# A matrix product with a subtraction: rings of slots for loads and stores, listed transfers, and a second DMA queue

## The chip, the cores and the metric

The kernel runs on one core of one Trainium2 chip. The metric is the device time of one execution, in microseconds (us). Each core has five engines that run their own instruction streams in order: PE (TensorE, matrix products and transposes), DVE (VectorE), ACT (ScalarE), POOL (GpSimd) and SP (SyncE, which here only issues DMA transfers). The transfers themselves are carried out by the core's 16 DMA engines.

## The reference

```python
def setup_inputs():
    batch, m, k, n = 16, 512, 1024, 768
    return {
        "x": np.random.randn(batch, m, k).astype(np.float32),
        "weight": np.random.randn(k, n).astype(np.float32),
        "sub_value": np.random.randn(batch, m, n).astype(np.float32),
    }

def reference(x, weight, sub_value):
    return (np.matmul(x, weight) - sub_value).astype(np.float32)
```

Flattened, this is a product of 8192 x 1024 by 1024 x 768, less a matrix of 8192 x 768, all in float32. Through the DMA engines go x (33.6 MB), the weight (3.1 MB), sub (25.2 MB) and the output (25.2 MB), 87 MB in all.

## The kernel before

**Tiles.** The 8192 rows are cut into 64 m tiles of 128 rows. Eight m tiles make a block of 1024 rows: partition p of tile j of the block holds row 8p + j. So the rows of several neighbouring m tiles lie next to one another in memory, and one transfer of n tiles moves, for each partition, one contiguous row of n times 4 KB (x) or n times 3 KB (sub, out).

**One m tile's way.** The x tile arrives in float32. ACT casts it to float16 (`cast`, L99). Most tiles are then transposed by PE: four 128 x 128 transposes, in which a pair of float16 travels as one float32 (L116), and ACT copies the transposed tile from PSUM to SBUF (L123, called the xt copy below). The seven pairs of tiles whose first number is in `ON_DVE` (18, 24, 30, 36, 42, 48, 54) are transposed by DVE instead, 16 block transposes for a pair (L137). Then PE does 16 matmuls for a tile (L149), four for each of the four slices c of the inner dimension, into one of three PSUM buffers. DVE subtracts the sub tile from the PSUM buffer and writes the result over the sub tile in SBUF (`finish`, L160). The output is stored from there.

**Order of the work.** All instructions are kept in the order in which the program writes them, on each engine. The main loop (L218) runs over m tiles from 3 on. In the iteration of tile mi, PE does the matmuls of mi with the four transposes of tile mi + 2 between them, and ACT's copy of that tile follows. Then come the casts that are due: a tile of a DVE pair is cast seven tiles ahead, another four tiles ahead. Then `finish(mi)`, and, when a DVE pair comes up in six tiles, its 16 transposes are put on a list of which four are issued per iteration. So on ACT, the cast of a tile of a DVE pair stands before the xt copies of nearer tiles. The first three tiles are interleaved with the arrival of the four weight slices; idle matmuls (L177) fill the waits there.

**Transfers.** All transfers are issued on SP's queue. x lies in four buffers of four tiles each, sub and out in seven buffers of four tiles each (the weight's staging takes four of these first). The head is a written list: x tiles and weight slices, one by one, then x and sub by turns, one or two tiles each (L23). From then on the loop issues at each fourth tile an x load three groups ahead, a sub load two groups ahead and the store of the group two back, each of four tiles. A load waits on SP until the buffer that it fills is free, and every later transfer is behind it. The last group is stored in pieces of two, one and one tile (L244 to L246).

SP has eight completion semaphores for its transfers, which are used in rotation: each issue also waits until the transfer eight issues before it has landed.

## Time and profile before

| | |
|---|---|
| median of 8 runs | 213.15 us |
| lowest and highest | 212.65, 213.8 us |
| the profiled execution's own time | 212.65 us |
| its span, first to last instruction | 210.8 us |
| granted TensorE clock in it | 0.992 |
| moved by DMA | 87.23 MB, mean 414 GB/s |
| data and other packets | 9374, of them 1040 under 512 B |

The profile is of one execution. Its span is 1.85 us shorter than its time. Engine times in it are sums of busy time; waiting, branching and the issue of DMAs don't count as busy. A timeline line gives the start in us from the span's start, the duration, the engine (SPq is SP's queue), the line of the kernel, the operation, the tiles written and read, the shape, how many instructions were merged, and in brackets the idle time before with what ended it. A wait for several things is put down to the one that came last.

The transfers by kind, with the size of one and the median time from issue to landing:

```profile
x_tile<-in_x_dram SPq DMA_DIRECT2D x13, 2048.0 KB, 31.1
out_dram<-so_tile SPq DMA_DIRECT2D x15, 1536.0 KB, 31.9
so_tile<-in_sub_value_dram SPq DMA_DIRECT2D x14, 1536.0 KB, 33.0
```

A transfer issued in the middle of the kernel lands some 30 us later: it stands behind those issued before it.

### The profile page before, as it was taken

What the parts mean: (1) busy time and instruction counts of PE and PEld (TensorE: products, weight loads), DVE (VectorE), ACT (ScalarE), POOL (GpSimd) and SP (SyncE); (2) the same over time, 40 slices, a digit from 0 to 9 for tenths busy, and PEclk for the clock granted to TensorE, in tenths of its full rate; (3) what the DMA queues carried; (4) which work ended last, traced back from release to release, by engine and by line L of the source; (5) the groups of instructions that cost most, each with busy time, mean ns of one, the idle gap of its engine ahead of it and who ended that gap; (6) DMA issues with size and microseconds to landing.
All of it is one profiled execution on the core that took longest, in us unless ns stands there. A gap on an engine that the chain in (4) does not pass through costs nothing.

```text
span 210.8 us, 3028 instructions
## 1 busy us (share of the span) xinstructions
PE 198.5 (94%) x1249; PEld 129.9 (62%) x1249; DVE 114.0 (54%) x186; ACT 112.7 (53%) x115; POOL 0.7 (0%) x6
## 2 busy tenths in 40 slices
PE   7999799999999999999989999998999999999960
PEld 2455566776666775776656566664656666776630
DVE  0343313152598299389519939941993994133330
ACT  3646666757842847465086555509645553557300
POOL 1000000000000000000000000000000000000000
PEclk9999999999999999999999999999999999999996
DMA  6999999999999999999999999999999999999994
GB/s 222 423 410 410 414 417 446 415 426 434 420 434 417 429 429 419 438 427 430 421 431 436 425 437 411 438 423 426 431 429 429 417 438 417 425 417 434 422 414 175
DMA packets 9374, 87.23 MB, mean 414 GB/s; under 512 B 1040, under 2 KB 1040, under 8 KB 3728
## 3 DMA queue, kind: packets, MB, share of 16 engines
q1 hardware_dynamic: 9360, 87.04, 98.3%
q8 instruction: 10, 0.16, 0.3%
q14 instruction: 4, 0.03, 0.0%
HBM read 61.87 MB, written 25.17 MB: 413 GB/s over the span
## 4 chain that ended last, share of the span: by engine, by line
DMA 49%; PE 33%; ACT 9%; DVE 3%; SPq 1%; issue 1%; ACTq 0%
DMA x_tile<-in_x_dram 49%; PE psum_o L149 28%; PE psum_t L116 5%; ACT x_tile L108 4%; ACT xt_tile L123 3%; ACT x16p_tile L105 2%; DVE xtp_tile L137 2%; DVE so_tile L160 1%; SPq L79 1%; SPq L87 1%; ACTq L105 0%
## 5 line engine op out<-in xcount | busy, mean ns | idle before, releaser
L149 PE MATMUL psum_o<-w_sb,xt_tile 128*128 128x384 f16 x800 | 146.0, 326 | 1.6 <-ACT xt_tile L123 1.6
L149 PEld LDWEIGHTS <-xt_tile 128*128 128x128 f16 x800 | 78.2, 98 | 41.8 <-ACT xt_tile L123 2.7
L160 DVE TENSOR_TENSOR so_tile<-psum_o,so_tile 128x768 f32<-128x768 f32 x64 | 60.7, 956 | 57.4 <-PE psum_o L149 39.6
L123 ACT COPY xt_tile<-psum_t 128x1024 f16<-128x1024 f16 x50 | 50.6, 1012 | 59.5 <-PE psum_t L116 58.7
L137 DVE STREAM_TRANSPOSE xtp_tile<-x16p_tile 32x256 f32<-32x256 f32 x112 | 48.8, 436 | 22.2 <-ACT x16p_tile L105 20.5
L108 ACT CAST x_tile<-x_tile 128x1024 f16<-128x1024 f32 x50 | 51.7, 1048 | 6.6 <-DMA x_tile<-in_x_dram 6.5
L116 PE MATMUL psum_t<-ident,x_tile 128*128 128x128 f32 x200 | 52.4, 274 | 2.0 <-ACT x_tile L108 1.4
L149 PE MATMUL psum_o<-w_sb,xtp_tile 128*128 128x384 f16 x224 | 42.9, 326 | 0.6 <-DVE xtp_tile L137 0.6
L116 PEld LDWEIGHTS psum_t<-ident,x_tile 128*128 128x128 f32 x200 | 27.6, 141 | 16.0 <-ACT x_tile L108 4.3
L149 PEld LDWEIGHTS <-xtp_tile 128*128 128x128 f16 x224 | 21.8, 98 | 10.9 <-DVE xtp_tile L137 1.4
L105 ACT CAST x16p_tile<-x_tile 128x1024 f16<-128x1024 f32 x14 | 14.7, 1047 | 20.3 <-DMA x_tile<-in_x_dram 20.3
L81 DVE CAST w_sb<-w_stage 128x768 f16<-128x768 f32 x8 | 4.1, 556 | 10.5 <-DMA w_stage<-in_weight_dram 10.5
L177 PE MATMUL psum_o<-idle_x,idle_w 128*128 128x512 f16 x25 | 8.3, 486 | 1.3 <-DVE idle_x L172 1.3
L177 PEld LDWEIGHTS <-idle_w 128*128 128x128 f16 x25 | 3.0, 118 | 5.0 <-issue 3.2
L108 ACT ACT_TABLE_LOAD x1 | 1.3, 1283 | 0.7 <-PEq L261 0.7
L171 DVE MEMSET idle_w<- 128x64 uint32 x1 | 0.1, 112 | 0.8 <-PEq L261 0.8
masks.py:199 POOL TENSOR_SCALAR_AFFINE_SELECT ident<-ident 128x128 f32<-128x128 f32 x1 | 0.3, 292 | 0.1
L172 DVE MEMSET idle_x<- 128x256 uint32 x1 | 0.3, 272 | 0.0
masks.py:197 POOL MEMSET ident<- 128x128 f32 x1 | 0.2, 204 | 0.3 <-POOLq L261 0.3
L261 POOL MEMSET const-bfloat16-1.0<- 128x1 bf16 x1 | 0.1, 101 | 0.0
L261 POOL MEMSET const-uint8-127<- 128x1 uint8 x1 | 0.1, 101 | 0.0
L261 POOL MEMSET const-float32-0.0<- 128x1 f32 x1 | 0.1, 98 | 0.2 <-issue 0.2
(1 smaller groups left out, 0.1 us busy)
## 6 DMA issues: line engine op xcount, KB each, us to landing
x_tile<-in_x_dram SPq DMA_DIRECT2D x13, 2048.0 KB, 31.1
out_dram<-so_tile SPq DMA_DIRECT2D x15, 1536.0 KB, 31.9
so_tile<-in_sub_value_dram SPq DMA_DIRECT2D x14, 1536.0 KB, 33.0
x_tile<-in_x_dram SPq DMA_DIRECT2D x8, 512.0 KB, 10.5
w_stage<-in_weight_dram SPq DMA_DIRECT2D x4, 768.0 KB, 8.7
x_tile<-in_x_dram SPq DMA_DIRECT2D x2, 1024.0 KB, 12.7
so_tile<-in_sub_value_dram SPq DMA_DIRECT2D x4, 384.0 KB, 11.0
so_tile<-in_sub_value_dram SPq DMA_DIRECT2D x2, 768.0 KB, 13.3
```

What stands on the lines that cost most here:

```text
L79: keep(nc.sync.dma_start(out=st, in_=w_c[c]))
L81: keep(nc.vector.tensor_copy(out=w_sb[:, c, r], in_=st[:, r]))
L87: keep(nc.sync.dma_start(out=x_t[g][:, j : j + n], in_=rows(x_s, mi, n)))
L105: keep(nc.scalar.copy(out=x16_t["pair", first][:, mi - first], in_=x_t[g][:, j]))
L108: keep(nc.scalar.copy(out=x16_t[mi], in_=x_t[g][:, j]))
L116: keep(nc.tensor.transpose(ps_t[mi].bitcast(F32)[:, c * P : (c + 1) * P], x16_t[mi].bitcast(F32)[:, c * P : (c + 1) * P], ident,))
L123: keep(nc.scalar.copy(out=xt_t[mi], in_=ps_t.pop(mi)))
L137: keep(nc.vector.transpose(xt[b * Q : (b + 1) * Q, :, a * Q : (a + 1) * Q], x16[a * Q : (a + 1) * Q, :, b * Q : (b + 1) * Q],))
L149: keep(nc.tensor.matmul(po_t[mi][:, h, :NS], xt_t[mi][:, 2 * P * c + r : 2 * P * (c + 1) : 2], w_sb[:, c, r, h * NS : (h + 1) * NS], start ...
L160: keep(nc.vector.tensor_tensor(out=o, in0=po_t.pop(mi)[:, :, :NS], in1=o, op=mybir.AluOpType.subtract))
L177: keep(nc.tensor.matmul(idle_o[:, 0], idle_w, idle_x, start=True, stop=True))
L261: nc = _bacc.Bacc("TRN2", target_bir_lowering=False, num_devices=1)
```

## The change

x gets one ring of 16 slots, and sub with out one ring of 32 slots, in place of buffers of four tiles. All loads stand in one list, with up to eight tiles in a transfer. A function `issue` goes through the list: it issues the load at the front if, in the order in which the program is written, the former users of its slots have been written down (for x, the casts of the tiles 16 before; for sub, the stores of the tiles 32 before), and stops at the first that has not. It is called at the start and after each cast, finish and store. The waits for the data itself are put in as before.

Stores stand in a second list: each entry says after which tile's iteration it is issued, from which tile on, and how many tiles. They are issued on ACT's queue; loads stay on SP's. The weight slices are staged in slots 24 to 31 of the second ring. The computing instructions of PE, DVE and ACT and their order are as before.

```diff
-G = 4
-XA, SA, OA = 3, 2, 2
+NX, NSO = 16, 32
...
-HEAD_TRANSFERS = [('x', 0, 1), ('w', 0, 0), ('x', 1, 1), ('w', 1, 0), ('x', 2, 1), ('w', 2, 0), ('w', 3, 0), ('x', 3, 1), ('s', 0, 1), ('x', 4, 1), ('s', 1, 1), ('x', 5, 1), ('s', 2, 1), ('x', 6, 1), ('s', 3, 1), ('x', 7, 1), ('x', 8, 2), ('s', 4, 2), ('x', 10, 2), ('s', 6, 2)]
+
+LOADS = [
+    ('x', 0, 1), ('w', 0, 1), ('x', 1, 1), ('w', 1, 1), ('x', 2, 1), ('w', 2, 1),
+    ('w', 3, 1), ('x', 3, 2), ('s', 0, 1), ('x', 5, 3), ('s', 1, 3), ('x', 8, 3),
+    ('s', 4, 4), ('x', 11, 5), ('s', 8, 8), ('x', 16, 8), ('x', 24, 3), ('s', 16, 8),
+    ('x', 27, 5), ('s', 24, 8), ('x', 32, 8), ('s', 32, 8), ('x', 40, 8), ('s', 40, 8),
+    ('x', 48, 8), ('s', 48, 8), ('x', 56, 8), ('s', 56, 8),
+]
+
+STORES = [(18, 0, 8), (26, 8, 8), (34, 16, 8), (42, 24, 8), (50, 32, 8), (54, 40, 8), (58, 48, 8), (61, 56, 4), (63, 60, 2), (63, 62, 1), (63, 63, 1)]
...
+    x_ring = x_pool.tile([P, NX, K], F32)
+    so_ring = so_pool.tile([P, NSO, N], F32)
...
+    todo = list(LOADS)
+    done = {"w": set(), "x": set(), "s": set(), "o": set(), "cast": set(), "finish": set()}
+
+    def issue():
+        while todo:
+            kind, at, n = todo[0]
+            span = set(range(at, at + n))
+            old = {t - NX if kind == "x" else t - NSO for t in span}
+            need, by = {
+                "w": (set(), "o"),
+                "x": ({t for t in old if t >= 0}, "cast"),
+                "s": ({t for t in old if t >= 0}, "o"),
+            }[kind]
+            if not need <= done[by]:
+                return
+            todo.pop(0)
+            done[kind] |= span
+            if kind == "w":
+                first = NSO - 2 * (n_c - at)
+                st = so_ring[:, first : first + 2]
+                keep(nc.sync.dma_start(out=st, in_=w_c[at]))
+                for r in range(2):
+                    keep(nc.vector.tensor_copy(out=w_sb[:, at, r], in_=st[:, r]))
+                continue
+            ring, size, view = (x_ring, NX, x_s) if kind == "x" else (so_ring, NSO, sub_s)
+            keep(nc.sync.dma_start(
+                out=ring[:, at % size : at % size + n], in_=view[at // S][:, at % S : at % S + n]
+            ))
+
+    def store(at, n):
+        assert set(range(at, at + n)) <= done["finish"]
+        done["o"] |= set(range(at, at + n))
+        keep(nc.scalar.dma_start(
+            out=out_s[at // S][:, at % S : at % S + n], in_=so_ring[:, at % NSO : at % NSO + n]
+        ))
+        issue()
...
-        g, j = divmod(mi, G)
-        if j == 0 or mi == HEAD:
-            if g + XA < n_g:
-                load_x((g + XA) * G, G)
-            if g + SA < n_g:
-                load_sub((g + SA) * G, G)
-            if g >= OA:
-                store((g - OA) * G, G)
...
-    for g in range(n_g - OA, n_g - 1):
-        store(g * G, G)
-    store(n_mt - G, G - 2)
-    store(n_mt - 2, 1)
-    store(n_mt - 1, 1)
+        for after, at, n in STORES:
+            if after == mi:
+                store(at, n)
+    assert not todo
```

`cast` and `finish` read the rings (`x_ring[:, mi % NX]`, `so_ring[:, mi % NSO]`) in place of the buffers, and call `issue` at their end.

## The prediction

> **What bounds the kernel now.** I read the share of busy time first, then the chain of waits, then windows of the span, then the ACT, DVE, PE and SP timelines at the few places where PE is late. PE is busy 94% of the span, yet the chain gives half of it to one kind of DMA:

> ```profile
> PE 198.5 (94%) x1249; PEld 129.9 (62%) x1249; DVE 114.0 (54%) x186; ACT 112.7 (53%) x115; POOL 0.7 (0%) x6
> DMA 49%; PE 33%; ACT 9%; DVE 3%; SPq 1%; issue 1%; ACTq 0%
> 16.00:22.50 6.50, 4.96 (x31) 2.74 (x29) 2.72 (x3) 4.95 (x5) 0.00 (x0) 1.00 1.03 404
> 180.00:200.00 20.00, 20.00 (x133) 13.89 (x132) 6.70 (x7) 11.82 (x12) 0.00 (x0) 1.00 1.01 426
> 206.00:208.00 2.00, 0.00 (x0) 0.00 (x0) 0.00 (x0) 0.00 (x0) 0.00 (x0) 0.82 0.78 315
> ```

> The windows' last two columns are the DMA engines' busy share and GB/s. The DMA engines are full from about 2 us to 206 us, at 404 GB/s with 3 and 4 KB rows and near 428 later. PE is full as well. So two resources are bound together, and the order of transfers decides who waits. The places where PE is late:

> ```profile
> 69.35 1.05 ACT L105 CAST x16p_tile<-x_tile 128x1024 f16<-128x1024 f32 x1 [4.75 <-DMA x_tile<-in_x_dram]
> ...
> 106.22 1.05 ACT L105 CAST x16p_tile<-x_tile 128x1024 f16<-128x1024 f32 x1 [6.93 <-DMA x_tile<-in_x_dram]
> ...
> 142.81 1.05 ACT L105 CAST x16p_tile<-x_tile 128x1024 f16<-128x1024 f32 x1 [7.16 <-DMA x_tile<-in_x_dram]
> 143.76 1.01 ACT L123 COPY xt_tile<-psum_t 128x1024 f16<-128x1024 f16 x1
> 144.66 1.05 ACT L108 CAST x_tile<-x_tile 128x1024 f16<-128x1024 f32 x1
> 145.61 1.05 ACT L105 CAST x16p_tile<-x_tile 128x1024 f16<-128x1024 f32 x1
> ```
> ```profile
> 146.69 1.78 DVE L137 STREAM_TRANSPOSE xtp_tile<-x16p_tile 32x256 f32<-32x256 f32 x4 [4.92 <-ACT x16p_tile L105]
> ...
> 155.06 1.79 DVE L137 STREAM_TRANSPOSE xtp_tile<-x16p_tile 32x256 f32<-32x256 f32 x4
> ```
> ```profile
> 144.82 0.83 PE L149 MATMUL psum_o<-w_sb,xt_tile 128*128 128x384 f16 x4 [0.90 <-ACT xt_tile L123]
> ...
> 156.91 0.82 PE L149 MATMUL psum_o<-w_sb,xtp_tile 128*128 128x384 f16 x4 [0.30 <-DVE xtp_tile L137]
> ```

> This is the mechanism on which I build. The cast of the first tile of a DVE pair (18, 24, ... 54) is issued seven tiles early and sits in ACT's order before an xt copy. When its x tile is late, ACT stands still. From the start of cast 48 (142.81), PE gets tile 44 at 144.82, 2.0 us later, and the pair's tile 48 at 156.91, 14.1 us later (the second cast, then 16 DVE transposes spread over four tiles). The same holds for pair 36: 106.22 and 14.1 are 120.3, where PE waits another 0.30.

> The three casts also give the landing line. They end the waits for x 24-27, 36-39 and 48-51. Counting the transfers in issue order (x 0.524 MB a tile, sub and out 0.393, a weight slice 0.786) these are bytes 27.26, 42.99 and 58.72 MB: 73.46 us for 31.46 MB, 2.33 us per MB, so a landing is at 69.35 + 2.33 x (MB - 27.26). SP's own timeline confirms it: each issue waits for the landing eight issues before, and x 20-23 (22.02 MB, by the line 57.1) releases:

> ```profile
> 57.19 0.34 SPq L97 DMA_DIRECT2D out_dram<-so_tile  x1
> ```

> For pair 18 the line leaves room today, since x 16-19 are in at 18.35 MB (48.5 us) and the cast runs in its turn:

> ```profile
> 50.40 1.05 ACT L108 CAST x_tile<-x_tile 128x1024 f16<-128x1024 f32 x1
> 51.35 1.05 ACT L105 CAST x16p_tile<-x_tile 128x1024 f16<-128x1024 f32 x1
> 52.53 1.01 ACT L123 COPY xt_tile<-psum_t 128x1024 f16<-128x1024 f16 x1
> ```
> ```profile
> 66.64 0.81 PE L149 MATMUL psum_o<-w_sb,xtp_tile 128*128 128x384 f16 x4
> ```

> [...]

> **The change part by part.**

> *Fewer, longer packets.* 65 DMAs become 39 (28 loads, 11 stores), so 26 x 128 rows of packets go. An engine's time for a packet: at 404 GB/s 25.25 B/ns, so a 3.5 KB packet takes 142 ns; at 428 a mean of 13.65 KB takes 510 ns; the line through both has 10.7 ns per packet that don't depend on size. A removed DMA (8 packets an engine) is worth at most 0.086 us[...]. I take 0.07: 1.8 us at the end.

> *Head.* x 3 comes with x 4: 0.524 MB more before it lands, 1.25 us at 2.4 us per MB. ACT's chain cast 3, copy, cast 4, copy, cast 5 is serial, so transposes of tile 5 go from 22.56 to 23.8. x 5-7 land near 22.1, in time. sub 1-3 land as one near 26, so finish(1) and with it PE's third output buffer can cost up to 0.6 more. Head: +1.25 to +1.85; what follows overrides it.

> *x 16-23.* The list puts sub 8-15 ahead and brings eight tiles as one transfer. It ends at 22.02 MB: 57.1, less 9 removed DMAs x 0.07, 56.5. Cast 18 waits for it instead of running at 51.35 plus the head. By the chain of pair 48, PE gets tile 14 at 58.5 (before, 55.4) and tile 18 at 56.5 + 14.1 = 70.6 (before, 66.64): PE is 4.0 us late.

> *Middle.* x 24-26, 27-31, 32-39 (39.85 MB, 97.9) and 40-47 (50.33 MB, 122.2) are in before their casts, so the waits before 69.35 and 106.22 go, and PE's stalls of 0.67 (at 107.6) and 0.30 (at 120) with them: PE is 3.0 us late.

> *x 48-55.* It waits for cast 39 (tile 35, near 121), behind sub 40-47, and out 16-23 has been put on ACT's queue after tile 34 and shares the engines. All of these are through before it: 60.82 MB in place of 58.72 for x 48-51. The line gives 147.7, less 19 x 0.07: 146.4. Cast 48 at 146.5 gives tile 44 at 148.5 and tile 48 at 160.6 (before, 156.91): PE is 3.7 us late. Behind cast 48 on ACT also stands the store of out 24-31. From there PE has no gap before, so it ends at 203.93 + 3.7 = 207.6.

> *SP's order.* sub 32-39 waits on SP for the landing of out 0-7, with x 40-47 behind it. Out 0-7 goes out near 77 and at half share lands near 94; SP has x 32-39 in flight until 98, so nothing idles. Later rounds have 4 to 10 us of cover. Gone, it would idle the engines one for one.

> *sub in eights.* sub 8-15 lands as one at 17.83 MB, 47.3 less 0.5: 46.8. finish(8) ends at 47.8, and PE, with three output buffers, needs that one for tile 11 at 48.2: hidden, with 0.4 to spare. sub 40-47 lands near 137.5, when finish(40) is due; two tiles (6 us) of buffers cover it. If that cover went, PE would wait one for one.

> *ACT's issues.* 11 of 0.3 to 0.5 us, on an engine idle for half the time: nothing but in the tail. Their eighth-earlier DMAs have landed long before.

> *Tail.* Loads end early, so only stores remain, and out 48-55 is issued on ACT after tile 58's cast 62. That cast ended at 191.6 before, so 195.3. The engines run dry: what is queued ends near 193 (slowest engine) or 190 (fastest). Behind that issue are 16 tiles, 6.29 MB, 14.7 us. A transfer from cold costs 2.66 us besides its bytes (first x: issued 0.74, landed 4.63, 1.23 of bytes). 195.3 + 2.66 + 14.7 = 212.7, and up to 0.9 for a second gap before out 56-59 (issued near 203.6); I take 0.45: 213.1. PE's own path, 207.6 + 0.96 + 0.3 + 2.66 + 0.9 = 212.4, is just inside. Before, the last landing is at 209.8 (issued by 205.28, SP waits 4.4).

> *Sum.* +3.3 us on 210.8 and on the 212.65 of the profiled execution: 215.9. That execution was the fastest of the eight; against the median 213.15 it is 216.4.

> **Rivals.**
> *Loads outrun stores.* If SP's longer rows get most of the engines, x 48-55 is in time. PE keeps 4.0 less the stalls that go (0.67, 0.30, 0.90, 0.30): 1.8 late. The tail's issue is at 193.4: +1.4, 214.5. [...] Against: out 16-23 has 25 us to get through.
> *Two queues cost more.* If the engines lose 2% from 77 us on, x 48-55 is 1.4 later and the last stores 0.3: 218.1. An issue on ACT that held ACT would look alike. Nothing in the profile shows it.
> *Faster.* One mechanism: x 16-23 lands before cast 18 is due (51.35 plus the head, by 53.2), so tile 18 is not held, and without the stalls of 2.2 PE ends 0.4 early: tail issue 191.2, last landing 209.0, 212.3. It decides at 3.3 us in the first 56.5, some 6% of rate. [...] an absent lag of the slowest engine might give half.
> *The rings don't do it.* If a load waited for every user of a ring, transfers and casts would be serial: far over 250. Against: today's finish(0) runs at 18.5 while tile 3 of the same buffer lands at 24.9.

> **How the numbers follow.** Forecast 216.4 with 0.50 (own range 215.2 to 217.8), loads outrun stores 0.20, two queues cost more 0.20, faster 0.08, rings 0.02. About 0.2% can be told from no change, 0.4 us. Faster 0.08, same 0.06 (the low end of the loads that outrun stores and the rest of the faster case's neighbourhood), slower 0.86. Low 213.4 takes in that rival with the removed DMAs at their upper price; high 219.3 the costly queues, with the second gap before the stores counted in full and removed DMAs at nothing.

> **What would show it.** A wait of cast 18 for x ending at 56 to 57, tile 18 near 70.6; a wait of cast 48 ending near 146.5; no wait at casts 24 and 36; the DMA share under 0.9 between 190 and 197. Wrong if cast 18 finds its x by 53, if the DMA stays full to the end, or if sub tiles, not x, hold PE.

## Result, and the profile after

The changed kernel takes 216.31 us at the median (215.64 to 217.82, 11 runs) against 213.15 us before. The ratio is 1.0159, with a 95% interval of 1.0143 to 1.0174: slower by 1.6%. (It is the ratio of the means; the two medians give 1.0148, and the forecast of 216.4 over the median before gives 1.0152.) The profiled execution took 215.66 us, one of the fastest of these runs, with a span of 213.8 us (the forecast's sum was 214.1). The longer executions had the lower granted clock: those with a mean of 0.992 of full speed took 215.64 to 216.32 us, those with 0.987 took 216.37 to 217.12, and those with 0.978 and 0.979 took 217.66 and 217.82.

The page of the changed kernel, parts 1, 4 and 6 (engines' busy time; the chain that ended last; transfers with the median time to landing):

```profile
PE 199.5 (93%) x1249; PEld 130.6 (61%) x1249; DVE 114.0 (53%) x186; ACT 112.5 (53%) x115; POOL 0.7 (0%) x6
...
PE 54%; DMA 32%; ACT 6%; DVE 3%; issue 2%; SPq 1%; ACTq 0%
...
out_dram<-so_ring ACTq DMA_DIRECT2D x7, 3072.0 KB, 19.0
x_ring<-in_x_dram SPq DMA_DIRECT2D x5, 4096.0 KB, 26.8
```

PE and DVE do the same work as before. Less of the chain runs over DMA (49% to 32%) and more over PE (33% to 54%), which fits an end that PE's lateness sets. The last subtraction, before and after:

```profile
203.96 0.96 DVE L160 TENSOR_TENSOR so_tile<-psum_o,so_tile 128x768 f32<-128x768 f32 x1 [1.64 <-PE psum_o L149]
...
209.01 0.96 DVE L190 TENSOR_TENSOR so_ring<-psum_o,so_ring 128x768 f32<-128x768 f32 x1 [1.64 <-PE psum_o L178]
```

It starts 5.05 us later, yet the span is only 3.0 us longer: before, stores still took 6.84 us from there to the end of the span, now 4.79.

A store of twice the size lands in 19.0 us, where it took 31.9 in the single queue: on ACT's queue it doesn't stand behind the loads. An estimate with an equal share of the engines for each queue is twice its 7.4 us of bytes (2.33 us per MB) and the 2.7 of a cold transfer, 17.5; that the shares are equal is an assumption, which no run shows.

ACT's timeline at the two places named in the forecast:

```profile
56.27 1.05 ACT L133 CAST x16p_tile<-x_ring 128x1024 f16<-128x1024 f32 x1 [3.17 <-DMA x_ring<-in_x_dram]
57.22 1.00 ACT L152 COPY xt_tile<-psum_t 128x1024 f16<-128x1024 f16 x1
...
147.30 1.04 ACT L133 CAST x16p_tile<-x_ring 128x1024 f16<-128x1024 f32 x1 [9.53 <-DMA x_ring<-in_x_dram]
147.40 0.34 ACTq L120 DMA_DIRECT2D out_dram<-so_ring  x1
148.25 1.00 ACT L152 COPY xt_tile<-psum_t 128x1024 f16<-128x1024 f16 x1
```

These are casts 18 and 48. Both wait for x, and the xt copies of tiles 14 and 44, which PE needs at once, stand right behind them. PE's timeline, at tile 14, tile 18 and tile 44:

```profile
58.28 0.82 PE L178 MATMUL psum_o<-w_sb,xt_tile 128*128 128x384 f16 x4 [1.10 <-ACT xt_tile L152]
...
70.41 0.82 PE L178 MATMUL psum_o<-w_sb,xtp_tile 128*128 128x384 f16 x4 [0.35 <-DVE xtp_tile L166]
...
149.31 1.46 PE L178 MATMUL psum_o<-w_sb,xt_tile 128*128 128x384 f16 x4 [3.26 <-ACT xt_tile L152]
...
150.78 1.49 PE L178 MATMUL psum_o<-w_sb,xt_tile 128*128 128x384 f16 x4
152.22 0.81 PE L178 MATMUL psum_o<-w_sb,xt_tile 128*128 128x384 f16 x4
```

Besides the two gaps there is something the forecast did not have: after the gap of 3.26 us, four matmuls take 1.46 and 1.49 us instead of 0.81. The windows show why (the number before the last two is the granted clock):

```profile
144.00:147.00 3.00, 2.05 (x14) 1.24 (x12) 0.00 (x0) 0.00 (x0) 0.00 (x0) 1.00 1.01 434
147.00:150.00 3.00, 0.69 (x3) 0.36 (x4) 0.00 (x0) 2.70 (x3) 0.00 (x0) 0.79 1.01 434
150.00:153.00 3.00, 3.00 (x15) 1.83 (x14) 1.75 (x5) 3.00 (x4) 0.00 (x0) 0.64 1.03 442
...
190.00:197.00 7.00, 7.00 (x49) 4.89 (x47) 1.92 (x2) 4.50 (x5) 0.00 (x0) 1.00 0.61 260
```

In shorter windows the clock is at one half from 148.8 to 152.2 us: it falls during the pause and is still low when PE starts again. The last line is the tail: the DMA engines are busy 61% between 190 and 197 us, where before they were full.

### The profile page after: what moved, and what is told of

It is laid out like the page before. It is cut to its first block, busy times and chain, and to the rows that moved or that the text cites. A ratio compares the mean times of both kernels' runs of the same rounds, so it can differ in the third digit from the quotient of the medians.

```text
span 213.8 us, 2970 instructions
## 1 busy us (share of the span) xinstructions
PE 199.5 (93%) x1249; PEld 130.6 (61%) x1249; DVE 114.0 (53%) x186; ACT 112.5 (53%) x115; POOL 0.7 (0%) x6
## 4 chain that ended last, share of the span: by engine, by line
PE 54%; DMA 32%; ACT 6%; DVE 3%; issue 2%; SPq 1%; ACTq 0%
PE psum_o L178 48%; DMA x_ring<-in_x_dram 32%; PE psum_t L145 7%; ACT x_tile L136 3%; ACT xt_tile L152 2%; DVE xtp_tile L166 2%; DVE so_ring L190 1%; SPq L108 1%; ACT x16p_tile L133 1%; SPq L113 1%; ACTq L120 0%; ACTq L133 0%; ACTq L152 0%
## 5 line engine op out<-in xcount | busy, mean ns | idle before, releaser
L190 DVE TENSOR_TENSOR so_ring<-psum_o,so_ring 128x768 f32<-128x768 f32 x64 | 60.6, 956 | 60.0 <-PE psum_o L178 42.7
L136 ACT CAST x_tile<-x_ring 128x1024 f16<-128x1024 f32 x50 | 51.6, 1048 | 6.4 <-DMA x_ring<-in_x_dram 6.3
L133 ACT CAST x16p_tile<-x_ring 128x1024 f16<-128x1024 f32 x14 | 14.6, 1046 | 17.1 <-DMA x_ring<-in_x_dram 17.1
L110 DVE CAST w_sb<-so_ring 128x768 f16<-128x768 f32 x8 | 4.1, 556 | 10.5 <-DMA so_ring<-in_weight_dram 10.5
```

Source lines behind the costliest of these rows:

```text
L110: keep(nc.vector.tensor_copy(out=w_sb[:, at, r], in_=st[:, r]))
L133: keep(nc.scalar.copy(out=x16_t["pair", first][:, mi - first], in_=x_in))
L136: keep(nc.scalar.copy(out=x16_t[mi], in_=x_in))
L190: keep(nc.vector.tensor_tensor(out=o, in0=po_t.pop(mi)[:, :, :NS], in1=o, op=mybir.AluOpType.subtract))
```

## The experiments

All are compared with the kernel before on the same chip (medians there 212.72 and 212.74 us), so ratios are what to set beside the changed kernel's 1.0159. Unless said otherwise an experiment is an edit of the changed kernel.

**The first late transfer alone.**

```diff
-    ('s', 8, 8), ('x', 16, 8),
+    ('s', 8, 4), ('x', 16, 4), ('s', 12, 4), ('x', 20, 4),
```

> Edit: in the list of loads, sub 8-15 and x 16-23 go in fours, by turns (sub 8-11, x 16-19, sub 12-15, x 20-23), as before the change. The rest is as in the changed kernel. Theory (the later lateness covers the earlier): x 16-19 lands near 48, cast 18 doesn't wait, PE is some 2 us earlier at tile 18 than in the changed kernel, but then waits some 5 us instead of 3.3 for the xt copy of tile 44, since x 48-55 lands at 147 as before. Time 216.3, within 0.4. Rival (each lateness adds): PE's gain at tile 18 is kept to the end: 213 to 214.

215.69 us, ratio 1.0134 (1.0105 to 1.0164), by the ratios 0.5 us below the changed kernel, with intervals that overlap. Cast 18 no longer waits, and the gap at tile 14 is gone. But tile 44 is late again, for the same transfer:

```profile
149.06 1.46 PE L178 MATMUL psum_o<-w_sb,xt_tile 128*128 128x384 f16 x4 [3.13 <-ACT xt_tile L152]
...
150.53 1.49 PE L178 MATMUL psum_o<-w_sb,xt_tile 128*128 128x384 f16 x4
...
152.03 1.49 PE L178 MATMUL psum_o<-w_sb,xt_tile 128*128 128x384 f16 x4
...
153.52 1.49 PE L178 MATMUL psum_o<-w_sb,xt_tile 128*128 128x384 f16 x4
```

Tile 44 starts at 149.06 against 149.31: what PE gained at tile 18 (1.8 us, 68.62 against 70.41) is lost, as the first theory had it. The time lies between the two expected ranges, 0.2 us below the theory's. The gap is 3.1 us and not 5, because smaller waits (0.69 at 127, 0.30 at 139) came before it. The slow matmuls last twice as long in this execution.

**The store in front of x 48-55.**

```diff
-STORES = [(18, 0, 8), (26, 8, 8), (34, 16, 8), ...
+STORES = [(18, 0, 8), (26, 8, 8), (38, 16, 8), ...
```

> Edit: the store of out 16-23 is issued after tile 38 instead of after tile 34; one number of the changed kernel. Theory (x 48-55 is late because out 16-23 on the other queue goes through before it): 3.15 MB less stand before x 48-55, 7 us, so it lands near 140 and cast 48 doesn't wait. The gap of 3.3 us before tile 44 goes, and so do the slow matmuls after it (1.3 us). The last subtraction starts near 204.4 instead of 209.0, time 211.5 to 213. Rival (the transfers' sum or the dry DMA engines at the end set the time): 216, whatever PE does.

212.84 us, ratio 1.0012 (0.9994 to 1.0029): one number takes nearly the whole loss away. ACT's and PE's timelines:

```profile
144.96 1.05 ACT L133 CAST x16p_tile<-x_ring 128x1024 f16<-128x1024 f32 x1 [6.61 <-DMA x_ring<-in_x_dram]
```
```profile
146.97 0.82 PE L178 MATMUL psum_o<-w_sb,xt_tile 128*128 128x384 f16 x4 [0.34 <-ACT xt_tile L152]
```

The time is in the expected range and the slow matmuls are gone. But cast 48 still waits for x 48-55, until 144.96 and not near 140, and the last subtraction starts at 206.11 in the profiled execution, not near 204.4. Out 16-23 is issued at 132.4, while x 48-55 is in flight, and presumably still takes a share of the engines.

**The second transfer, in fours; the first left late.**

```diff
-    ('s', 40, 8), ('x', 48, 8),
+    ('s', 40, 4), ('x', 48, 4), ('s', 44, 4), ('x', 52, 4),
```

> Edit: in the changed kernel, only sub 40-47 with x 48-55 go in fours by turns; x 16-23 stays one transfer behind sub 8-15. Theory (the earlier lateness, some 3 us at tile 18, is partly made good in the middle, where the kernel before waited too): the cast of tile 18 waits as in the changed kernel, the gap before tile 44 is under 0.5 us, the last subtraction starts at 204 to 206, the time is 212 to 213. Rival (tile 18's lateness is all kept): the last subtraction starts at 207.5 or later, 214 or more.

212.31 us, ratio 0.9978 (0.997 to 0.9986). Cast 18 waits until 56.6 as in the changed kernel, the gap before tile 44 is gone, and the last subtraction starts at 204.51:

```profile
139.16 1.05 ACT L133 CAST x16p_tile<-x_ring 128x1024 f16<-128x1024 f32 x1 [1.07 <-DMA x_ring<-in_x_dram]
...
204.51 0.96 DVE L190 TENSOR_TENSOR so_ring<-psum_o,so_ring 128x768 f32<-128x768 f32 x1 [1.64 <-PE psum_o L178]
```

The first line is cast 48. So the second transfer is most of the loss (1.0159 to 0.9978), and with tile 18's lateness left in, the kernel is no slower than the one before.

**Both transfers in fours.** The two edits above together.

> Edit: in the changed kernel's list of loads, sub 8-15 with x 16-23, and sub 40-47 with x 48-55, go in fours by turns; nothing else. Theory (two late x transfers are all of the loss): x 16-19 lands near 48, x 48-51 near 140, no gap of PE over 0.5 us after 27 us, the granted clock stays at 1 in the middle, the last subtraction starts at 203.5 to 205, and the time is 210.5 to 212.3, below the kernel before. Rival (rings, eights and the second queue cost something besides): 213.5 or more.

211.60 us, ratio 0.9948 (0.9927 to 0.9968): faster than the kernel before. Its windows:

```profile
147.00:150.00 3.00, 3.00 (x22) 2.12 (x20) 2.86 (x7) 1.34 (x2) 0.00 (x0) 1.00 0.97 418
150.00:153.00 3.00, 3.00 (x21) 1.94 (x19) 2.91 (x6) 1.50 (x2) 0.00 (x0) 1.00 0.95 410
190.00:197.00 7.00, 7.00 (x48) 4.89 (x46) 2.39 (x3) 4.10 (x5) 0.00 (x0) 1.00 1.00 428
```

After 28 us PE has no gap over 0.31 us, its clock stays full, and the DMA engines are full from 190 to 197, with the stores listed at the very same tiles: in the changed kernel they run dry there because PE's lateness delays the issues. The last subtraction starts at 203.48, 1.0 us before that of the kernel with the second transfer alone in fours. So the first transfer is worth some 0.3% (0.9978 to 0.9948), about what it gave alone (1.0159 to 1.0134). Rings, eights elsewhere and the second queue together are no loss.

**Stores earlier in the tail.**

```diff
-(54, 40, 8), (58, 48, 8), (61, 56, 4)
+(52, 40, 8), (56, 48, 8), (60, 56, 4)
```

> Edit: the stores of out 40-47, 48-55 and 56-59 are issued after tiles 52, 56 and 60 instead of 54, 58 and 61. Theory (PE's lateness sets the end): the DMA engines have less idle time between 190 and 206, but the last tile is still subtracted at 209 and its store is alone on the engines, so the last landing moves by 0 to 0.4 us: 215.9 to 216.4. Rival (holding the stores back costs the time): the engines' idle time of some 3 us between 190 and 204 comes off the end: 213 to 214.

215.75 us, ratio 1.0135 (1.0115 to 1.0155), 0.2% below the changed kernel with intervals that overlap, and just under the expected 215.9. The engines' idle time only moves (windows of this kernel):

```profile
190.00:197.00 7.00, 7.00 (x48) 4.93 (x47) 2.45 (x3) 4.84 (x6) 0.00 (x0) 1.00 0.98 421
...
200.00:206.00 6.00, 6.00 (x42) 4.10 (x40) 1.91 (x2) 2.78 (x3) 0.00 (x0) 1.00 0.58 244
```

They are full until 197 and then wait for PE's last tiles. From the last subtraction to the end of the span it is 4.23 us here, 4.79 in the changed kernel, and 4.16 at the least in any run (`all_x40`). So while PE is this late, earlier stores can take off some 0.6 us at most; the rest of the loss is PE's.

**One queue.** The changed kernel with its stores on SP's queue.

```diff
-        keep(nc.scalar.dma_start(
+        keep(nc.sync.dma_start(
```

> Edit: the changed kernel with its stores issued on SP's queue at the same places of the program, so that all transfers stand in one queue. Theory (the order of bytes matters, not the number of queues): x 48-55 still has 60.8 MB up to its end and lands at 146 to 148; time 215.5 to 217. Rival (a second queue costs or gives something of itself[...]): more than 1 us away from 216.3, 214.5 or lower if it costs.

219.54 us, ratio 1.0316 (1.0302 to 1.0331). The first theory fell: the number of queues matters. SP's timeline and the window:

```profile
96.23 0.33 SPq L113 DMA_DIRECT2D x_ring<-in_x_dram  x1
96.61 0.43 SPq L120 DMA_DIRECT2D out_dram<-so_ring  x1
122.37 0.33 SPq L113 DMA_DIRECT2D so_ring<-in_sub_value_dram  x1
122.75 0.43 SPq L120 DMA_DIRECT2D out_dram<-so_ring  x1
123.28 0.37 SPq L113 DMA_DIRECT2D x_ring<-in_x_dram  x1
```
```profile
120.00:140.00 20.00, 20.00 (x130) 13.22 (x129) 15.27 (x27) 10.35 (x11) 0.00 (x0) 1.00 0.88 338
```

With one queue, out 8-15 stands behind x 40-47. Sub 40-47 must wait on SP for its landing, and x 48-55 and the next store stand behind that wait. By 122.4 nothing else is in flight, so the engines run dry (nothing moves from 121 to 123 us, 338 GB/s in the window shown). Cast 48 then waits until 151.6, and PE's gap is 7.37 us. In the changed kernel the store of out 16-23 goes out on ACT at 117.6, whatever SP waits for. So with this plan of transfers the second queue is worth some 1.5%.

**The second queue in the kernel before.** The reverse edit: the kernel before, with its stores on ACT's queue.

```diff
-        keep(nc.sync.dma_start(out=rows(out_s, mi, n), in_=so_t[g][:, j : j + n]))
+        keep(nc.scalar.dma_start(out=rows(out_s, mi, n), in_=so_t[g][:, j : j + n]))
```

> Edit: the kernel before, with its stores issued on ACT's queue in place of SP's, nothing else. Theory (a store on the other queue overtakes the loads that are queued, so one store of 1.57 MB more is through before a given x tile lands): casts 36 and 48 wait up to 3.7 us longer than in the kernel before, PE is some 2 to 3 us later, 214.5 to 216.5. Rival (the number of queues is without effect while the engines are full): 212.3 to 213.3.

217.13 us, ratio 1.0208 (1.0181 to 1.0235), more than expected. ACT's timeline has it at cast 24, which the expectation did not name:

```profile
76.71 1.04 ACT L105 CAST x16p_tile<-x_tile 128x1024 f16<-128x1024 f32 x1 [10.30 <-DMA x_tile<-in_x_dram]
```

That cast ran at 69.35 before: x 24-27 is 7.4 us later, as much as two stores of 1.57 MB take, where I had counted one; out 4-7 and out 8-11 were issued on ACT at 52.20 and 62.58, before it landed. PE stands still for 4.38 us and restarts with slow matmuls. So a second queue lets stores overtake loads, and whether that helps hangs on the list: good where a load waits for a store, bad where PE waits for a load.

**The pause and the clock.** In the changed kernel, idle matmuls before those of tile 44, in the same PSUM buffer:

```diff
             po_t[mi] = psum_o_pool.tile([P, 2, 512], F32, name="psum_o")
+            if mi == 44:
+                for _ in range(14):
+                    keep(nc.tensor.matmul(po_t[mi][:, 0], idle_w, idle_x, start=True, stop=True))
```

> Edit: the changed kernel with 14 idle matmuls of 512 columns, some 3 us, before the matmuls of tile 44, into the same PSUM buffer, which the real matmuls then overwrite. PE has nothing else to do there. Theory (the granted clock falls to 0.5 after a pause of about 3 us, for 2 to 6 us, and makes PE 0.9 to 2.4 us later): the clock stays at 1 between 144 and 156, the last subtraction starts at 208 to 208.5 instead of 209 to 210, and the time is 0.7 to 1.5 us lower, 214.8 to 215.3. Rival (the slow clock is covered by other waits, such as DVE's transposes of pair 48): within 0.3 of the changed kernel.

215.32 us, ratio 1.0117 (1.0098 to 1.0135), some 0.9 us below the changed kernel by the ratios, within the 0.7 to 1.5 that were expected. PE's timeline:

```profile
146.30 3.19 PE L178 MATMUL psum_o<-idle_x,idle_w 128*128 128x512 f16 x14
149.34 0.82 PE L181 MATMUL psum_o<-w_sb,xt_tile 128*128 128x384 f16 x4
...
150.44 0.81 PE L181 MATMUL psum_o<-w_sb,xt_tile 128*128 128x384 f16 x4
```

Tile 44 starts no earlier (149.34), but its matmuls run at once at full speed, and the last subtraction starts at 208.48 instead of 209.01. The slow restart is thus a cost of its own, caused by PE's pause. From the start of tile 44 to the last subtraction PE takes 59.14 us here, 59.70 in the changed kernel and 61.18 in `x16_fours`: by the profiles the slow restart costs 0.6 us, or 2.0 where it lasts twice as long.

**Further on from both in fours.** `all_four` takes both transfers in fours, the head's x 3 to 5 apart, and earlier stores; `all_x40` also takes sub 32-39 and x 40-47 in fours.

```diff
-    ('w', 3, 1), ('x', 3, 2), ('s', 0, 1), ('x', 5, 3), ('s', 1, 3), ('x', 8, 3),
+    ('w', 3, 1), ('x', 3, 1), ('x', 4, 1), ('s', 0, 1), ('x', 5, 1), ('s', 1, 1), ('x', 6, 2), ('s', 2, 2), ('x', 8, 3),
...
-(54, 40, 8), (58, 48, 8), (61, 56, 4), (63, 60, 2), (63, 62, 1)
+(52, 40, 8), (56, 48, 8), (60, 56, 4), (61, 60, 2), (62, 62, 1)
```

And in `all_x40` alone:

```diff
-    ('s', 32, 8), ('x', 40, 8),
+    ('s', 32, 4), ('x', 40, 4), ('s', 36, 4), ('x', 44, 4),
```

> Edit: both pairs of transfers in fours, x 3 and x 4 apart and x 5, sub 1 alone in the head, and the stores of the last 24 tiles issued earlier (40-47 after tile 52, 48-55 after 56, 56-59 after 60, 60-61 after 61, 62 after 62). Theory: PE gains the head's 1.3 us besides and the engines hardly run dry before 204; what stays is the sum of transfers, less the 1.5 us that longer packets save: 210 to 211.5. Rival (PE's head doesn't matter and DMA had slack): as both_fours within 0.3.

> Edit: all_four, with sub 32-39 and x 40-47 in fours by turns as well. Theory (in both_fours and all_four the sum of the transfers on the slowest DMA engine already sets the end, at 208.6): the 3 us gap of PE at 125 goes and the last subtraction starts near 202.5 to 203.5, but the last landing stays at 208.3 to 208.8; time 211.2 to 211.7. Rival (PE sets the end): the landing follows PE by 2 us, 210 or lower.

`all_four`: 211.63 us, ratio 0.9938 (0.9921 to 0.9954), just above what was expected and no different from both in fours, as the rival had it, but not for the rival's reason. PE's head is 2.0 us faster, but x 40-47 is now too late for it, and PE pauses 2.97 us at 125. `all_x40`: 214.23 us, ratio 1.0065 (1.0037 to 1.0093). Both expectations missed. The gap at 125 went, and ACT's and PE's timelines show a new one:

```profile
175.56 1.04 ACT L136 CAST x_tile<-x_ring 128x1024 f16<-128x1024 f32 x1 [8.26 <-DMA x_ring<-in_x_dram]
```
```profile
173.05 0.83 PE L178 MATMUL psum_o<-w_sb,xtp_tile 128*128 128x384 f16 x4 [1.65 <-DVE xtp_tile L166]
176.66 0.33 PE L145 MATMUL psum_t<-ident,x_tile 128*128 128x128 f32 x1 [2.79 <-ACT x_tile L136]
```

Now x 56-63 is late. With PE ahead, the stores, whose places are tied to PE's tiles, go out earlier (out 32-39 at 163.21, in `all_four` at 167.56) and take their share from the next load. That this is the reason was not tried by itself.

## Why the prediction was right, point by point

- **Longer packets.** x 16-23 releases cast 18 at 56.27; the forecast had 56.5, the landing line before 57.1. Right in sign and near in size (56.47 to 56.86 in the five other runs with this part of the list). The profile counts 144 packets for each transfer in both kernels (9360 for 65, 5616 for 39), so rows of 24 and 32 KB count as one packet each.
- **Head.** Transposes of tile 5 start at 23.8, as worked out. The wait for an output buffer was 0.23 us, inside the 0 to 0.6; in other runs with this head it was 0.30 to 0.95. At 30 us PE is 1.64 us behind the kernel before (forecast 1.25 to 1.85).
- **x 16-23.** Tile 14 at 58.28 (forecast 58.5), tile 18 at 70.41 (70.6). In the forecast's chain x 48-55 takes this lateness's place; `x16_fours` and `x48_fours` show it.
- **Middle.** No wait at casts 24 and 36, as said. Cast 42 did wait, until 124.82: x 40-47 landed 2.6 us later than the line gave (122.2), presumably because out 16-23, issued at 117.6, shared the engines with its last part. PE did not feel it. By tile 44 PE was due at 146.05, 2.1 us later than before (143.92), not 3.0. That term was mis-sized: by the starts of the same transposes on PE, the changed kernel is 3.78 us behind from tile 18 on, 2.61 after the earlier kernel's wait at 107.6, and 2.13 after its wait at 120. So these two waits were worth 1.17 and 0.48 us, where the forecast took the idle time in the brackets, 0.67 and 0.30.
- **x 48-55.** Cast 48 at 147.30 (146.5), tile 44 at 149.31 (148.5). Shown as the cause by `o16_hold` and `x48_fours`: each takes over 3 us off. The landing is 0.8 us later than the forecast's.
- **From there to PE's end.** The forecast said that PE has no further loss. The trace and `warm44` show one: the slow clock after the pause. The last subtraction starts 5.05 us late (209.01 against 203.96), not 3.7: of the 1.35 us between, 0.8 come from x 48-55 itself and some 0.55 from the slow clock.
- **Tail.** The forecast put the issue of out 48-55 behind cast 62. It comes 0.09 us after the start of the copy of tile 60, while the cast still waits in ACT's turn:

```profile
194.70 1.01 ACT L152 COPY xt_tile<-psum_t 128x1024 f16<-128x1024 f16 x1 [1.08 <-PE psum_t L145]
194.79 0.34 ACTq L120 DMA_DIRECT2D out_dram<-so_ring  x1
195.61 1.05 ACT L136 CAST x_tile<-x_ring 128x1024 f16<-128x1024 f32 x1
```

That is 1.9 us earlier than after the cast, which ends at 196.66. It cancels PE's 1.35 us of extra lateness, so the sum of 214.1 for 213.8 is better than its terms; that two misses cancel here is luck. PE's own path was taken as 4.8 us from the last subtraction to the landing, which is too long: the span of `all_x40` ends 4.16 us after it. Neither the early issue nor the slow clock was in the forecast; the clock fell to a half after PE's pauses of 3.26 us here, 3.13 in `x16_fours` and 2.97 in `all_four`.
- **Rivals.** Loads did not outrun stores. For that case, x 48-55 in time, the forecast had PE 1.8 us late and 214.5; `x48_fours` brings the same about in another way and shows PE 0.55 us late (204.51) and 212.3: that term was too large. PE is 4.10 us late at tile 18 there, so the four waits of the kernel before were worth 3.55 us, not the 2.17 of the brackets. A second queue did not cost of itself but was worth about 1.5% with this list (`after_sp`), and it cost 2% in the kernel before (`before_act`). That a changed list of loads would be faster than the kernel before was not in the forecast's faster case, which asked for a rate of DMA some 6% higher up to 56.5 us (the engines moved 408 GB/s up to there, 403 in the kernel before); four tiles in place of eight in two places did it.

Left open: in what shares the two queues are served when both are full. The half share in the forecast was an assumption of mine. The store's 19.0 us is not far from the 17.5 estimated with it, but no run measured it by itself.

## What to carry to other kernels

When DMA and compute are both full, ask of each large transfer how many bytes are through before its last one, stores on the other queue included, and when its first tile is needed: a transfer of eight tiles makes its first tile as late as its last (cast 48 ran at 147.30 with x 48-55 in one transfer, at 139.16 with two in `x48_fours`). A later wait can take back what an earlier repair gained on PE: here tile 18 came 1.8 us sooner and tile 44 only 0.25. A store tied to PE's progress moves with every repair. A wait of PE can cost more than the idle time that the profile gives for it (1.17 us for 0.67 at 107.6 in the kernel before); compare the starts of the same instructions in two kernels. The second queue added no bandwidth to full engines (427 GB/s from 22.5 to 190 us in the kernel before, 426 in the changed one; 427 from 140 to 160 us in `before_act`); it let one kind of transfer pass another, which freed a waiting queue in one kernel (cast 48 at 147.30 against 151.6 in `after_sp`) and robbed an urgent load in the other (cast 24 at 76.71 in `before_act` against 69.35).
